# A ring of its own for the convolution LayerNorm's row tiles in a hybrid decoder layer

## The chip, the cores and the metric

The kernel runs on one core of a Trainium2 chip. The metric is the device time of one execution in microseconds (us). The engines are TensorE (PE), VectorE (DVE), ScalarE (ACT), GpSimd (POOL) and SyncE (SP); SP and POOL also issue DMAs. Each engine works through its own queue in order.

## The reference

One sequence of 4096 tokens with 1024 channels goes through one layer, in float32:

```
shift, scale, gate = split(silu(c) @ w_ada + b_ada)
h = layer_norm(x) * (1 + scale) + shift
u_a, z_a, glu_b, z_b = split(h @ w_in + b_in)          # 512, 512, 1024, 512 channels
y_a = (pool(u_a) @ w_pool + b_pool) * ls_pool * silu(z_a)
v = glu_b[..., :512] * sigmoid(glu_b[..., 512:])
v = silu(layer_norm(causal_depthwise_conv_31(v)) * ln_conv_g + ln_conv_b)
y_b = (v @ w_pw + b_pw) * silu(z_b)
y = concat(y_a, y_b) @ w_out + b_out
out = layer_norm(2**0.25 * x + gate * y) * ln_post_g + ln_post_b
```

The convolution has 31 taps for each of 512 channels and reads the current and the 30 earlier tokens. Its LayerNorm runs over the 512 channels of a token.

## The kernel before, in words

The tokens are cut into 8 blocks of T = 512, called sb 0 to 7. Activations are kept with channels on the 128 partitions and tokens along a row, so a tile is [128, 512]. Each matmul product is made of three matmuls: weights and activations are split into a high part and a low part, and high x high, high x low and low x high are added (L346, L347, L348 of `inproj`; L723 to L725 in the pointwise stage; all on L747 in the output projection).

*Phase 1* (the loop at L485) normalises x and makes glu_b and half of z_b. For the next block, `row_stats` (L284) loads four token tiles of x, lets ACT form sums and sums of squares (`col_stats`, L270 and L271) into a tile `xcs` of 8 columns, lets POOL turn the second half into inverse roots (`inv_root`, L274 and L275) and calls `to_rows`: PE transposes the 8 columns into PSUM (tile `xcp`, L74), ACT copies them to a small tile `rows` in SBUF (L281), and SP stores this to DRAM (L282), from where it is read back as a broadcast to all partitions, `xbc` (L293). With it `norm_T` (L301, L303) on DVE and `mod_xT` (L312 on ACT, L313 on DVE) make the normalised x with channels on partitions, `x2`. PE then projects it (tiles p1_sb_n), ACT takes the sigmoid (sg, L464), and DVE multiplies (v, L466); v is stored to DRAM.

*Phase 2* (L534) loads x2 again (DMAs in POOL's queue, L341) and makes the pool mixer: projections p2z, p2u and p2b, window sums on DVE (us, pp).

*The convolution* (L591 to L655) works on v in blocks of one or two sb: (0), (1, 2), (3, 4), (5). All taps run on DVE (L609), channel group by channel group (m = 0 to 3), with accumulators `ca` and scratch `cx` from one ring of six buffers. When the first channel group of the next block has been written in the program, `conv_ln` (L621) of the block before is emitted at high priority: PE transposes the accumulators (tiles cl), ACT forms the statistics `ccs` (L270, L271), POOL the inverse roots (L274, L275), and the same `to_rows` makes rows of them (transpose `ccp`, copy L281). They go through DRAM to a broadcast `cbc` (L637), and DVE normalises the accumulators (L640, L641), which are stored; then the `ca` buffers are free again. Blocks 6 and 7 are "late units" (tiles la, lx, lv), two of which stand ahead of phase 3 and the others between its steps.

*Phase 3* (L689) splits the convolution's output (tiles vp) and the pool mixer's (ya) into high and low (a cast on ACT, L200, and a subtraction on DVE, L201), runs the pointwise projection (pw, L723 to L725), multiplies with z (L730), splits again (yb), and runs the output projection (po, L747) with the weights Wo (loaded and scaled at L784 to L790: DVE L787, ACT L200, DVE L201), then the last LayerNorm.

The program is not run in the order in which it is written. A scheduler walks it with a simulated timeline and puts each instruction into its engine's queue when its operands and buffers would be ready. A buffer comes from a ring: a tag with a number of buffers. A ring gives its buffers out in the order in which the program asks for them, so a tile that is asked for later in the program cannot have a buffer ahead of one that is asked for earlier. All of phase 1 stands ahead of the convolution in the program. The tile `rows` has the tag rows8 with two buffers in both uses of `to_rows`: for x (called with the name `x{sb}`) and for the convolution (called with `c{s0}`).

Of the kernel before, what the change touches and what calls it, by code (L numbers as in the profile page):

```python
# [9 lines left out]
F32 = mybir.dt.float32  # L10
# [7 lines left out]
P = 128  # L18
# [5 lines left out]
TT = T // P  # L24
# [16 lines left out]
def tile_layer(ctx, tc, x, x_t, w_in_t, c, w_ada, b_ada, w_in, b_in, w_pool, b_pool, ls_pool, w_dw, b_dw,  # L41
# [10 lines left out]
    def pool(name, bufs=1, **kw):  # L52
        return ctx.enter_context(tc.tile_pool(name=name, bufs=bufs, **kw))
# [4 lines left out]
    st = pool("st")  # L58
# [13 lines left out]
    def transpose(out_ap, in_ap):  # L72
        n = in_ap.shape[0]
        return nc.tensor.transpose(out_ap, in_ap, ident[:n, :n])  # L74
# [202 lines left out]
    def to_rows(pb, cs, dst, name):  # L277
        n = cs.shape[1]
        transpose(pb[:n, :P], cs)
        rows = st.tile([n, P], F32, tag="rows8", bufs=2, name=f"rows{name}", padded_shape=[4 * TT, P])  # L280
        nc.scalar.copy(rows, pb[:n, :P])  # L281
        nc.sync.dma_start(dst, rows)  # L282

    def row_stats(sb):  # L284
        cs = st.tile([P, 8], F32, tag="cs", bufs=2, name=f"xcs{sb}")
        for t in range(TT):
            i = sb * TT + t
            xt = x_early[t] if sb == 1 else load_x(i)
            col_stats(xt, D, cs[:, t : t + 1], cs[:, 4 + t : 5 + t])
        inv_root(cs[:, 4:8], D)  # L290
        to_rows(tp_bank(f"xcp{sb}"), cs, rD[sb], f"x{sb}")
        bc = ph.tile([P, 2, T], F32, tag="tm", bufs=5, name=f"xbc{sb}")
        nc.sync.dma_start(bc, rD[sb].rearrange("(a t) p -> a (t p)", a=2).partition_broadcast(P))  # L293
        return bc
# [101 lines left out]
    rows = {}  # L396
# [224 lines left out]
    def conv_ln(s0, n, ac):  # L621
        nq = n * TT
        cs = st.tile([P, 2 * nq], F32, tag="ccs", bufs=2, name=f"ccs{s0}", padded_shape=[P, 4 * TT])
        for q in range(nq):
            pb = s2_bank(f"cl{s0}_{q}")
            for m in range(MC):
                transpose(pb[:, m * P : (m + 1) * P], ac[m][:, q * P : (q + 1) * P])
            col_stats(pb, DH, cs[:, q : q + 1], cs[:, nq + q : nq + q + 1])
        inv_root(cs[:, nq : 2 * nq], DH)
        bcs = []  # L630
        to_rows(s2_bank(f"ccp{s0}"), cs, cD[s0][: 2 * nq, :], f"c{s0}")
        for j in range(2):
            if s0 < 6:
                bc = s2.tile([P, n * T], F32, tag="bc", bufs=2, name=f"cbc{s0}_{j}", padded_shape=[P, D])
            else:
                bc = wraw(f"cbc{s0}_{j}")[:, :T]
            nc.sync.dma_start(bc, cD[s0][j * nq : (j + 1) * nq, :].rearrange("q p -> (q p)").partition_broadcast(P))  # L637
            bcs.append(bc)
        for m in range(MC):
            nc.vector.tensor_tensor(ac[m], ac[m], bcs[0], op=ALU.add)  # L640
            nc.vector.scalar_tensor_tensor(ac[m], ac[m], lcg[:, m : m + 1], bcs[1], op0=ALU.mult, op1=ALU.mult)  # L641
            for i in range(n):
                nc.sync.dma_start(tD[m][s0 + i], ac[m].rearrange("p (two i) -> p two i", two=2)[:, :, i * TH : (i + 1) * TH])

    pend = None
    for s0, n in BLOCKS:
        ac = []
        for m in range(MC):
            v = s2.tile([P, 2, HQ + n * TH + 1], F32, tag="cv", bufs=2, name=f"cv{s0}_{m}",
                        padded_shape=[P, 2, HQ + T + 1])  # L650
            a = s2.tile([P, n * T], F32, tag="ca", bufs=6, name=f"ca{s0}_{m}", padded_shape=[P, 2 * (HQ + T + 1)])
            tmp = s2.tile([P, 2 * n * TH + HQ + 1], F32, tag="ca", bufs=6, name=f"cx{s0}_{m}",
                          padded_shape=[P, 2 * (HQ + T + 1)])
# [186 lines left out]
```

## Time and profile before

| | |
|---|---|
| median of 3 runs | 1421.36 us (1421.3 to 1422.22) |
| the profiled execution | 1421.22 us |
| its span in the profile | 1419.4 us |
| mean granted TensorE clock | 0.984 |
| HBM read, written | 156.65 MB, 86.04 MB |
| matmuls on PE | 6109 |

The profile shows one execution. The span goes from the first to the last instruction, and the profiled time is 1.8 us longer. Times in the rows are in us from the span's start. A timeline row has its start, its length, engine, line, operation, output and inputs with their shapes, how many instructions the row stands for, and in brackets how long the engine was idle before it and what ended that wait. A windows row has the stretch, its length, then busy time and instruction count of PE, PE's weight loads, DVE, ACT and POOL, then the granted PE clock (1.00 is full), the share of the DMA engines and GB/s.

### The profile page before, as it was taken

Reading aid. Unit: us, or ns where it says so; the run is one execution under the profiler, and the core shown is the slowest. Engines: PE = TensorE matmul, PEld = TensorE weight load, DVE = VectorE, ACT = ScalarE, POOL = GpSimd, SP = SyncE. Lnnn points to the kernel's source line nnn. Section 1 sums busy time; section 2 is a strip of 40 time slices with the busy share of each in tenths; the row PEclk is TensorE's granted clock in tenths of the full one; section 3 lists DMA queues with packets and bytes.
Section 4 is the critical chain, followed back from the end, with each engine's and each line's share of the span. In section 5 each row is a group of like instructions: output and inputs, shape, how many; then the busy total and the mean of one; then the engine's idle time right before and its main releaser. Section 6 shows DMA issues by size and latency. Waiting matters only on the chain.

```text
span 1419.4 us, 17051 instructions
## 1 busy us (share of the span) xinstructions
PE 1371.0 (97%) x6109; PEld 1129.2 (80%) x6109; DVE 1178.4 (83%) x2220; ACT 432.5 (30%) x772; POOL 115.5 (8%) x159
## 2 busy tenths in 40 slices
PE   5999998999999999999999999987999999999997
PEld 4878886888888888888888888865888888888886
DVE  7588998752419999899999699999998899998754
ACT  3623534245244221321111411243334231323310
POOL 1000003000000001011011010000111001001011
PEclk9999999999999999999999999998999999999999
DMA  9696556456567576164341461436344443343511
GB/s 317 220 313 236 214 187 235 173 208 219 189 233 269 170 220 215 45 203 141 124 157 63 157 212 39 143 122 234 134 149 163 164 155 115 134 154 109 200 63 75
DMA packets 116551, 243.82 MB, mean 172 GB/s; under 512 B 15154, under 2 KB 49778, under 8 KB 116466
## 3 DMA queue, kind: packets, MB, share of 16 engines
q1 hardware_dynamic: 107184, 209.15, 42.5%
q0 software_dynamic: 9216, 33.56, 7.2%
q8 instruction: 48, 0.79, 0.2%
q14 instruction: 37, 0.30, 0.1%
q10 hardware_dynamic: 66, 0.02, 0.0%
HBM read 156.65 MB, written 86.04 MB: 171 GB/s over the span
## 4 chain that ended last, share of the span: by engine, by line
PE 88%; DVE 5%; DMA 3%; ACT 1%; POOL 1%; SPq 1%; issue 1%; DVEq 0%; ACTq 0%; POOLq 0%
PE po L747 24%; PE p L346 7%; PE p L347 7%; PE p L348 7%; PE p2u L347 4%; PE p2z L347 4%; PE p2z L348 4%; PE p2u L348 4%; PE p2u L346 4%; PE p2z L346 4%; PE p2b L348 2%; PE p2b L347 2%; PE p2b L346 2%; PE pw L723 2%; PE pw L725 2%; PE pw L724 2%
## 5 line engine op out<-in xcount | busy, mean ns | idle before, releaser
L609 DVE SCALAR_TENSOR_TENSOR cx<-cv,wdw,cx 128x257 f32<-128x257 f32 (+1 forms) x240 | 145.0, 611 | 1.2
L609 DVE SCALAR_TENSOR_TENSOR ca<-cx,wsum,ca 128x256 f32<-128x256 f32 (+1 forms) x240 | 142.2, 608 | 0.0
L609 DVE SCALAR_TENSOR_TENSOR ca<-cv,wdw,ca 128x256 f32<-128x256 f32 (+1 forms) x224 | 133.9, 608 | 0.0
L466 DVE SCALAR_TENSOR_TENSOR v<-p,cols,sg 128x512 f32<-128x512 f32 x32 | 23.8, 745 | 71.9 <-ACT sg L464 68.9
L770 ACT ACTIVATE ojk<-r,osm 128x1024 bf16<-128x1024 f32 x31 | 35.7, 1151 | 153.4 <-DVE osm L767 153.4
L776 POOL TENSOR_TENSOR ors<-ove,mhalf 128x1 f32<-128x1 f32 x32 | 47.0, 1470 | 398.4 <-DVE ove L772 390.0
L341 POOL DMA_DIRECT2D x2r<-xD x64 | 34.9, 546 | 418.5 <-PE p2b L348 321.8
L539 ACT ACTIVATE sz<-p2z,cols 128x512 f32<-128x512 f32 x32 | 22.0, 688 | 121.8 <-PE p2z L348 113.1
L609 DVE SCALAR_TENSOR_TENSOR lx<-lv,wdw,lx 128x257 f32<-128x257 f32 x120 | 57.5, 479 | 0.0
L765 DVE SCALAR_TENSOR_TENSOR r<-po,r 128x512 f32<-128x512 f32 x62 | 40.6, 685 | 20.4 <-PE po L747 20.4
L609 DVE SCALAR_TENSOR_TENSOR la<-lx,wsum,la 128x256 f32<-128x256 f32 x120 | 57.3, 477 | 0.0
L312 ACT ACTIVATE x<-xk,shc 128x512 fp32r<-128x512 f32 x56 | 38.1, 719 | 59.0 <-DVE xk L303 59.0
L313 DVE SCALAR_TENSOR_TENSOR x<-xk,shc,x 128x512 fp32r<-128x512 f32 x56 | 40.1, 743 | 17.3 <-ACT x L312 17.3
L546 ACT ACTIVATE u<-p2u,bu 128x512 f32<-128x512 f32 x32 | 22.1, 690 | 105.2 <-PE p2u L348 105.2
L609 DVE SCALAR_TENSOR_TENSOR la<-lv,wdw,la 128x256 f32<-128x256 f32 x112 | 53.1, 478 | 0.0
L301 DVE TENSOR_TENSOR xk<-xk,xbc 128x1024 f32<-128x1024 f32 x28 | 34.1, 1218 | 21.8 <-DMA xk<-in_x_t_dram 17.7
L747 PE MATMUL po<-wo0h,ya 128*128 128x512 f32 x128 | 42.0, 400 | 8.6 <-ACT ya L200 8.6
L464 ACT ACTIVATE sg<-p,cols 128x512 f32<-128x512 f32 x32 | 22.0, 687 | 79.5 <-PE p L348 76.7
L200 ACT CAST yb<-z 128x512 fp32r<-128x512 f32 x32 | 19.8, 617 | 81.1 <-DVE z L730 66.4
L779 DVE SCALAR_TENSOR_TENSOR r<-r,ors,b_bc 128x1024 f32<-128x1024 f32 (+1 forms) x33 | 41.1, 1247 | 2.8 <-POOL ors L776 2.8
L747 PE MATMUL po<-wo2h,ya 128*128 128x512 f32 x128 | 40.0, 390 | 0.4 <-ACT ya L200 0.4
L747 PE MATMUL po<-wo1h,ya 128*128 128x512 f32 x128 | 40.3, 390 | 0.0
(378 smaller groups left out, 4107.1 us busy)
## 6 DMA issues: line engine op xcount, KB each, us to landing
x2r<-xD POOLq DMA_DIRECT2D x64, 512.0 KB, 7.5
xD<-x SPq DMA_DIRECT2D x56, 512.0 KB
x<-in_x_dram SPq DMA_DIRECT2D x32, 512.0 KB
r<-in_x_dram SPq DMA_DIRECT2D x32, 512.0 KB
out_dram<-r SPq DMA_DIRECT2D x31, 512.0 KB
xk<-in_x_t_dram SPq DMA_DIRECT2D x28, 512.0 KB
wa<-in_w_ada_dram SPq DMA_DIRECT2D x32, 256.0 KB
vD<-v SPq DMA_DIRECT2D x32, 256.0 KB
```

Source lines behind the costliest of these rows:

```text
L312: nc.scalar.activation(h2[:, 0, :], z, AF.Identity, bias=shc[:, k : k + 1])
L313: nc.vector.scalar_tensor_tensor(h2[:, 1, :], z, shc[:, k : k + 1], h2[:, 0, :].bitcast(F32), op0=ALU.add, op1=ALU.subtract)
L341: nc.gpsimd.dma_start(h2, xD[k][sb].bitcast(F32R))
L346: nc.tensor.matmul(ps, w[0], X[0], start=first, stop=False)
L347: nc.tensor.matmul(ps, w[0], X[1], start=False, stop=False)
L348: nc.tensor.matmul(ps, w[1], X[0], start=False, stop=last)
L609: nc.vector.scalar_tensor_tensor(dst, src, wt, dst, op0=ALU.mult, op1=ALU.add)
L747: mm = nc.tensor.matmul(po[h], lhs, Wo[k][wi][:, h * 512 : (h + 1) * 512], start=(k == 0 and wi == 0 and lhs is yh), stop=last)
L765: nc.vector.scalar_tensor_tensor(r[:, sl], po[h], 1.0, r[:, sl], op0=ALU.mult, op1=ALU.add, accum_out=sm[:, h : h + 1])
L770: nc.scalar.activation(jk, r, AF.Square, bias=sm[:, 2:3], accum_out=ss)
L776: nc.gpsimd.tensor_tensor(rs, ve, mhalf[:, 0:1], op=ALU.pow)
L779: nc.vector.scalar_tensor_tensor(r[:, sl], r[:, sl], rs, b_bc[:, sl], op0=ALU.mult, op1=ALU.add)
```

## The change

The tag of the tile `rows` takes the first letter of its name: `rowsx` for the statistics of x, `rowsc` for those of the convolution. Each has one buffer in place of two shared ones, so the SBUF that they take is the same.

```
@@ -277,7 +277,7 @@
     def to_rows(pb, cs, dst, name):
         n = cs.shape[1]
         transpose(pb[:n, :P], cs)
-        rows = st.tile([n, P], F32, tag="rows8", bufs=2, name=f"rows{name}", padded_shape=[4 * TT, P])
+        rows = st.tile([n, P], F32, tag=f"rows{name[0]}", bufs=1, name=f"rows{name}", padded_shape=[4 * TT, P])
         nc.scalar.copy(rows, pb[:n, :P])
         nc.sync.dma_start(dst, rows)
```

No instruction is added to the arithmetic or taken from it; the scheduler orders the program anew. Up to PE's row 1067 (in sb 4) its queue is the same; the following three places show what differs. In the names, the number behind the tile's own name is the block, and the last number is a running one.

On ACT, in sb 3 of phase 1 (rowsc0 are the rows of convolution block 0, rowsx4 those of x block 4):

```order
 L464 ACTIVATE sg3_1_1958<-p1_3_13_1909,cols_92 128x512
 L281 COPY rowsx4_1838<-xcp4_1836 8x128
+L281 COPY rowsc0_6701<-ccp0_6699 8x128
 L464 ACTIVATE sg3_2_2013<-p1_3_14_1964,cols_92 128x512
 L312 ACTIVATE x2_4_0_2073<-xk4_0_1843,shc_283 128x512
```

The copy of block 0's rows now stands behind that of x block 4; before, it stood directly behind the copy of x block 7 (rowsx7), in sb 6.

On DVE, in sb 4 of phase 1, from the product v4_1 on, before:

```order
L466 SCALAR_TENSOR_TENSOR v4_1_2333<-p1_4_9_2281,cols_92,sg4_1_2331 128x512
L301 TENSOR_TENSOR xk5_0_2216<-xk5_0_2216,xbc5_2214 128x1024
L303 SCALAR_TENSOR_TENSOR xk5_0_2216<-xk5_0_2216,s1n_282,xbc5_2214 128x512 x2
L301 TENSOR_TENSOR xk5_2_2221<-xk5_2_2221,xbc5_2214 128x1024
L313 SCALAR_TENSOR_TENSOR x2_5_0_2446<-xk5_0_2216,shc_283,x2_5_0_2446 128x512
L301 TENSOR_TENSOR xk5_4_2462<-xk5_4_2462,xbc5_2214 128x1024
L466 SCALAR_TENSOR_TENSOR v4_2_2388<-p1_4_10_2336,cols_92,sg4_2_2386 128x512
```

And the same place now (ca1_1, cx1_1, ca1_2 and cx1_2 are the accumulators and scratch of convolution block 1):

```order
L466 SCALAR_TENSOR_TENSOR v4_1_2333<-p1_4_9_2281,cols_92,sg4_1_2331 128x512
L609 SCALAR_TENSOR_TENSOR cx1_1_6722<-cv1_1_6720,wdw_99,cx1_1_6722 128x513
L609 SCALAR_TENSOR_TENSOR ca1_1_6721<-cv1_1_6720,wdw_99,ca1_1_6721 128x512
L609 SCALAR_TENSOR_TENSOR ca1_2_6779<-cx1_2_6780,wsum_100,ca1_2_6779 128x512
L609 SCALAR_TENSOR_TENSOR cx1_2_6780<-cv1_2_6778,wdw_99,cx1_2_6780 128x513
L609 SCALAR_TENSOR_TENSOR ca1_2_6779<-cv1_2_6778,wdw_99,ca1_2_6779 128x512
L609 SCALAR_TENSOR_TENSOR ca1_1_6721<-cx1_1_6722,wsum_100,ca1_1_6721 128x512
```

Nine more taps follow before v4_2, so that fifteen stand between the two products; the first L301 of x block 5 now stands two taps behind v4_2. In the rest of phase 1 taps stand between the norm's instructions in the same way. On PE the transpose xcp5 moves from row 1164 to row 1189 (37 rows behind the last matmul of p1_4_9 and p1_4_13, whose products make v4_1), xcp6 and xcp7 stand at rows 1411 and 1649, and the transposes of the convolution's statistics move from row 2578 to 1982 (ccp1), 3411 to 2868 (ccp3), 4031 to 3466 (ccp5) and hardly for the two late blocks (4604 to 4582, 5560 to 5557). Phase 2 begins at row 2060 in place of 2027.

On PE, where phase 3 begins (pw0_0 and pw0_1 are the first pointwise projections, po0 the first output tile, cl6 a late unit's transpose), before:

```order
L723 MATMUL pw0_0_7802<-vp0_0_7705,wpw0h_7692 128x512
L723 MATMUL pw0_1_7821<-vp0_0_7705,wpw0h_7692 128x512
L74 MATMUL ccp5_7553<-ident_75,ccs5_7522 8x128
L74 MATMUL cl6_0_8676<-ident_75,la6_0_7574 128x128
L74 MATMUL cl6_1_8683<-ident_75,la6_0_7574 128x128
L724 MATMUL pw0_0_7802<-vp0_0_7705,wpw0h_7692 128x512
L725 MATMUL pw0_0_7802<-vp0_0_7705,wpw0l_7693 128x512
L724 MATMUL pw0_1_7821<-vp0_0_7705,wpw0h_7692 128x512
L725 MATMUL pw0_1_7821<-vp0_0_7705,wpw0l_7693 128x512
L747 MATMUL po0_0_7917<-wo0h_7745,ya0_0_7728 128x512
```

And now, from the last matmul of phase 2 on:

```order
L348 MATMUL p2b_7_3_6353<-x2r_7_7_6063,w19l_3628 128x512
L723 MATMUL pw0_0_7802<-vp0_0_7705,wpw0h_7692 128x512
L724 MATMUL pw0_0_7802<-vp0_0_7705,wpw0h_7692 128x512
L725 MATMUL pw0_0_7802<-vp0_0_7705,wpw0l_7693 128x512
L723 MATMUL pw0_0_7802<-vp0_1_7711,wpw0h_7692 128x512
L724 MATMUL pw0_0_7802<-vp0_1_7711,wpw0h_7692 128x512
L725 MATMUL pw0_0_7802<-vp0_1_7711,wpw0l_7693 128x512
L723 MATMUL pw0_0_7802<-vp0_2_7717,wpw1h_7698 128x512
```

The pieces of conv_ln(5) and of the late unit that stood among the first pw matmuls are gone from there, and the pw matmuls of one chunk follow each other.

More of the change, by code (lines that the diff above doesn't have):

```diff
@@ L279, in to_rows @@
         transpose(pb[:n, :P], cs)
-        rows = st.tile([n, P], F32, tag="rows8", bufs=2, name=f"rows{name}", padded_shape=[4 * TT, P])
+        rows = st.tile([n, P], F32, tag=f"rows{name[0]}", bufs=1, name=f"rows{name}", padded_shape=[4 * TT, P])
         nc.scalar.copy(rows, pb[:n, :P])
```

## The prediction

> **What bounds the kernel now.** The page comes first: the span, and what each engine is busy.
>
> ```profile
> span 1419.4 us, 17051 instructions
> PE 1371.0 (97%) x6109; PEld 1129.2 (80%) x6109; DVE 1178.4 (83%) x2220; ACT 432.5 (30%) x772; POOL 115.5 (8%) x159
> ```
>
> The profiled execution took 1421.22 us, 1.8 us more than its span and 0.14 us below the median 1421.36, so I sum against the span and add 1.8. PE is busy 97% of the time: a gain can only come from the 48 us in which it is idle and from stretches at a slow clock. The windows view says where these lie (columns: stretch, length, then PE, weight load, DVE, ACT, POOL busy with their instructions, PE clock, DMA share, GB/s).
>
> ```profile
> 225.00:250.00 25.00, 18.91 (x81) 14.90 (x80) 21.71 (x32) 12.01 (x28) 12.75 (x4) 0.89 0.52 183
> 300.00:400.00 100.00, 100.00 (x462) 83.16 (x461) 35.86 (x47) 35.62 (x59) 2.53 (x4) 1.00 0.59 213
> 925.00:950.00 25.00, 23.50 (x109) 19.30 (x107) 24.33 (x46) 11.48 (x22) 0.00 (x0) 1.00 0.37 117
> 950.00:975.00 25.00, 13.82 (x45) 9.52 (x45) 23.90 (x44) 6.87 (x14) 1.77 (x2) 0.66 0.70 230
> 975.00:1000.00 25.00, 22.16 (x88) 17.26 (x88) 23.73 (x51) 10.60 (x19) 0.00 (x0) 0.93 0.48 164
> 1228.34 21.78 PE po L747 x96
> 947.47 1.04 PE L74 MATMUL cl<-ident,ca 128*128 128x128 f32 x8
> ```
>
> The last row but one, from the chain that ended last, gives PE's full pace: 21.78 / 96 = 0.2269 us per 512-wide matmul; the last one, from PE's timeline, has eight small transposes in 1.04 us, an estimated 0.1 us each. The three slices from 925 to 1000, where phase 2 ends and phase 3 begins, hold 109 + 45 + 88 = 242 matmuls, 13 of them such transposes: 229 x 0.2269 + 1.3 = 53.2 us of work in 75. So 21.8 us are lost there: 25 x 3 - 23.50 - 13.82 - 22.16 = 15.5 idle, the rest slow clock (0.66 and 0.93 in the clock column). PE's timeline shows what it waited for (bracket: idle before, and its releaser), and DVE's what it did meanwhile:
>
> ```profile
> 950.78 0.98 PE L723 MATMUL pw<-vp,wpw0h 128*128 128x512 f32 x2 [2.28 <-ACT vp L200]
> 953.40 0.38 PE L74 MATMUL ccp<-ident,ccs 128*8 128x128 f32 x1 [1.64 <-POOL ccs L275]
> 964.93 1.22 PE L747 MATMUL po<-wo0h,ya 128*128 128x512 f32 x2 [8.62 <-ACT ya L200]
> 985.47 0.79 PE L723 MATMUL pw<-vp,wpw0h 128*128 128x512 f32 x1 [1.66 <-DVE z L730]
> 958.43 2.50 DVE L640 TENSOR_TENSOR ca<-ca,cbc 128x512 f32<-128x512 f32 x4 [0.36 <-DMA cbc<-cD]
> 964.22 2.73 DVE L641 SCALAR_TENSOR_TENSOR ca<-ca,lcg,cbc 128x512 f32<-128x512 f32 x4
> ```
>
> The 8.62 us wait is the largest. DVE is full there (23.90 of 25): the conv LayerNorm of block 5 (5.2 us in the last two rows) and taps stand in DVE's queue between PE and the splits (vp, ya) that it needs. Yet in 300 to 400 the same engine is busy for only 35.86 of 100 us, although conv taps were still to be done. Why, these rows show:
>
> ```profile
> 246.49 0.38 PE L74 MATMUL ccp<-ident,ccs 128*8 128x128 f32 x1 [4.50 <-POOL ccs L275]
> 412.98 0.26 ACT L281 COPY rowsx<-xcp 8x128 f32<-8x128 f32 x1 [3.31 <-PE xcp L74]
> 413.14 0.25 ACT L281 COPY rowsc<-ccp 8x128 f32<-8x128 f32 x1
> 421.88 2.49 DVE L640 TENSOR_TENSOR ca<-ca,cbc 128x512 f32<-128x512 f32 x4 [0.26 <-DMA cbc<-cD]
> ```
>
> Block 0's transposed statistics are ready at 246.5, but their copy to rows runs at 413.14, right behind that of x block 7: the shared ring hands buffers out in program order, and conv_ln(0) stands behind all of phase 1 there. Until 421.88 block 0's accumulators are not given back, and conv runs dry.
>
> **The change part by part.** *What goes.* With its own buffer rowsc0 is copied directly behind rowsx4, near 247 us. No arithmetic is added; the rings hold the same bytes. The conv taps fill DVE from about 250 on, and conv_ln runs earlier: ccp5 moves from PE's row 4031 to row 3466, 565 x 0.2269 = 128 us. In the new order the pw matmuls stand without a break behind phase 2, and nothing of conv_ln(5) or the late units stands around them on DVE. So the 21.8 us go, but for a rest: out projection still needs z through L730, a cast and a split (1.66 us above) and the Wo weights. I leave 2 us (0 to 5).
>
> *What earlier conv work buys elsewhere.* Nothing: PE is busy for all 25 us of every slice from 250 to 925, the first and last of which are
>
> ```profile
> 250.00:275.00 25.00, 25.00 (x109) 20.53 (x108) 16.56 (x25) 6.87 (x10) 0.00 (x0) 0.97 0.22 78
> 900.00:925.00 25.00, 25.00 (x112) 20.68 (x112) 24.97 (x51) 7.43 (x10) 0.00 (x0) 1.00 0.37 117
> ```
>
> The 6.1 us idle in 225 to 250 lie ahead of the first PE row that the change moves and stay.
>
> *What it adds.* From 300 to 425 the norm of x (L301 to L313) had DVE to itself; now it shares DVE with gapless 512-wide taps. Each x block's statistics pass through POOL (L274, L275) to a transpose in PE's queue; behind that transpose all of PE waits. The rows:
>
> ```profile
> 233.52 4.50 POOL L274 TENSOR_SCALAR xcs<-xcs 128x4 f32<-128x4 f32 x1 [60.34 <-ACT x L271]
> 237.86 0.75 DVE L466 SCALAR_TENSOR_TENSOR v<-p,cols,sg 128x512 f32<-128x512 f32 x1
> 239.20 0.27 PE L74 MATMUL xcp<-ident,xcs 128*8 128x128 f32 x1 [1.58 <-POOL xcs L275]
> 239.13 6.19 POOL L274 TENSOR_SCALAR ccs<-ccs 128x4 f32<-128x4 f32 x1
> 243.81 0.75 DVE L609 SCALAR_TENSOR_TENSOR ca<-cv,wdw,ca 128x512 f32<-128x512 f32 x1
> 244.48 0.75 DVE L609 SCALAR_TENSOR_TENSOR ca<-cx,wsum,ca 128x512 f32<-128x512 f32 x1
> 245.40 1.04 POOL L275 TENSOR_TENSOR ccs<-ccs,mhalf 128x4 f32<-128x4 f32 x1
> 246.52 0.77 PE L347 MATMUL p<-x,wg3h 128*128 128x512 f32 x1
> 251.36 0.40 PE L346 MATMUL p<-x,wg5h 128*128 128x512 f32 x1
> 300.31 0.23 POOL L274 TENSOR_SCALAR xcs<-xcs 128x4 f32<-128x4 f32 x1 [53.88 <-ACT x L271]
> ```
>
> L274 takes 0.23 us beside an idle DVE, but 4.50 and 6.19 inside streaks of 512-wide taps at 0.67 us pitch; the first ended when DVE ran an operation from PSUM (L466), the second when the streak ended at 245.2. PE lost 1.58 and 4.50 us, and after the longer one its 11 matmuls from 246.52 to 251.36 took 4.84 us for 11 x 0.2269 = 2.50: 2.3 more.
>
> Now xcs5. On ACT the last L271 of x block 5 now stands behind sg4_1, and xcp5 stands 37 PE rows, 8.4 us, behind the matmuls of that chunk. So POOL starts some 2.0 us behind the chunk (sg 0.69, L271 1.14 and its readout 0.19):
>
> ```profile
> 299.00 1.14 ACT L271 ACTIVATE x<-x,xcs 128x1024 f32<-128x1024 f32 x1
> 300.04 0.19 ACT L271 ACTIVATION_READ_ACCUMULATOR x<-x,xcs 128x1 f32 x1
> 301.43 0.69 ACT L464 ACTIVATE sg<-p,cols 128x512 f32<-128x512 f32 x1 [1.21 <-PE p L348]
> ```
>
> DVE runs v4_1 from 0.7 to 1.5 and then 15 taps without a break, 10 us, to 11.5. L274 ends there, L275 1.04 later, at 12.5: 4.1 us late, with the slow clock 6.4; if POOL gets in between two taps, 0. I take 5.
>
> The Trainium skill, SBUF — State Buffer, "SBUF: two separate sides", says that a DVE operation with two SBUF inputs and a GpSimd operation that reads SBUF take their shared ports as an exclusive lock, held for a whole instruction. By it POOL would enter behind one tap (0.75 us), xcs5 would cost nothing and the time would be 5 us less; 4.50 and 6.19 span seven and nine taps, so I go by the trace.
>
> xcs6 is ready some 4.5 us behind the chunk of v5_0, and xcp6 stands 47 rows, 10.7 us, behind that chunk; v5_1 comes between and lets POOL in: 0 to 1. xcs7 waits through 15 taps for v6_1, about 1.2 us behind its chunk, and takes L275's 1.04 more; xcp7 stands three rows, 0.7 us, behind that chunk: 1.5 to 2. ccs1 has ten us to its transpose, and among the splits of weights that wait for ACT's casts DVE has gaps: 0 to 1. The new rows are as late for norm_T as the transposes: before, from xcp5 (303.73) to x2_5_0's lo half took 12.0 us:
>
> ```profile
> 303.73 0.27 PE L74 MATMUL xcp<-ident,xcs 128*8 128x128 f32 x1
> 312.54 1.41 DVE L303 SCALAR_TENSOR_TENSOR xk<-xk,s1n,xbc 128x512 f32<-128x512 f32 x2
> 313.88 1.22 DVE L301 TENSOR_TENSOR xk<-xk,xbc 128x1024 f32<-128x1024 f32 x1
> 315.01 0.75 DVE L313 SCALAR_TENSOR_TENSOR x<-xk,shc,x 128x512 fp32r<-128x512 f32 x1
> ```
>
> Now 12 taps (8.0), two more L301 (2.3), three more L303 pairs (4.0) and v4_3 (0.7) stand ahead of it: 27.0. PE wants it 116 rows, 26.3 us, behind xcp5: 0 to 3, I take 1. At the start of phase 2 eight operations of conv_ln(1) stand ahead of v7_1, whose PSUM bank p2z waits for: 0 to 2, I take 1. POOL's queue now has conv_ln(1)'s pair between reloads 5 and 6 of the first x block, and SP's has its stores and broadcasts among phase 2's weight loads; what is queued behind them is first used at PE's row 2060, 78 rows or 17.7 us behind ccp1, which covers a wait of 6.19 on POOL: 0. Were that cover gone, it would be those 6 us.
>
> Sum: 5 + 2 + 1 + 1 = 9 us added, from 0 to about 20. Span 1419.4 - 21.8 + 2 + 9 = 1408.6, time **1410.4 us**.
>
> **The rivals.** *POOL decides (slower).* All four POOL pairs that now fall among taps (xcs5, xcs6, xcs7, ccs1) wait out a full streak: 6.19 + 2.3 = 8.5 us each, 34 in all, so 1421.2 - 21.8 + 2 + 34 = 1435 us. From 5 us per event up it eats the gain (19.8 / 4). For: two of two cases among 512-wide taps. Against: it needs each to start early in a streak and its transpose to stand close behind; by the order that holds for xcs5 only. 0.07.
>
> *The hole stays (same).* The 8.62 us wait names ya, but the Wo weights go into slots that phase 2's last chunks free, and if they come as late PE waits for them instead:
>
> ```profile
> 961.24 1.22 DVE L201 TENSOR_TENSOR wo7l<-wor,wo7h 128x1024 fp32r<-128x1024 f32 x1
> ```
>
> Then 8.62 + 2.3 of slow restart, 11 us, stay in place of my 2: 1410.4 + 9 = 1419.4, and up to 1424 where POOL costs 5 more than I took. For: wo7 is split at 961, next to that wait. Against: po begins with wo0, which was split earlier, and the splits now pass a DVE that is rid of 5.2 us of conv_ln and of the taps. 0.10.
>
> *Full gain.* POOL enters between the taps, as a 0.38 us L274 among 256-wide taps says:
>
> ```profile
> 171.60 0.38 POOL L274 TENSOR_SCALAR xcs<-xcs 128x4 f32<-128x4 f32 x1 [48.07 <-ACT x L271]
> ```
>
> Then only 0 to 3 us are added: 1400 to 1405. 0.20.
>
> *No effect.* If accumulators or another ring still held conv back, the order would not move; it does, by 128 us at ccp5. 0.01.
>
> **How the numbers follow.** The forecast has 0.62. A measurement can tell 0.2%, 2.8 us, from no change. The range, 1400 to 1422, has the full gain at its low end and the hole that stays at its high end; it leaves out POOL's 0.07, 0.05 of the hole's and the forecast's upper ends (20 us added) and 0.05 for a gain beyond 1400. Faster (below 1418.5): 0.62 + 0.20, less 0.02 of the forecast for its upper end: 0.80. Slower (above 1424.2): 0.07 and 0.03 of the hole's: 0.10. Same: the hole's other 0.07, the 0.02 and the 0.01: 0.10.
>
> **What would show it.** Right: rowsc0 copied near 247; DVE over 95% from 250 to 425; PE 24 or more of 25 in the slices where phase 2 ends, and no wait for ya or vp of over 2 us; a L274 of some 8 us near 303 to 313 with a PE wait of 4 for xcs behind it. Wrong: PE waits at the end of phase 2 adding up to over 8 us (the hole stays); each of the four L274 over 5 us with PE waits behind them (POOL decides); all of them under 1 us (full gain).

## The result and the profile after

The changed kernel takes 1410.78 us (median of 4 runs, 1409.85 to 1412.63) against 1421.33 for the kernel before on the same occasion (1421.22 to 1422.22): ratio 0.9926, with a 95% interval of 0.9909 to 0.9943. That is 10.6 us faster. The profiled execution took 1412.63 us, the longest of the four, 8.6 less than the profiled one of before; its span is 8.5 shorter. The page:

```profile
span 1410.9 us, 17053 instructions
PE 1370.4 (97%) x6109; PEld 1129.3 (80%) x6109; DVE 1181.7 (84%) x2220; ACT 435.7 (31%) x774; POOL 127.0 (9%) x159
```

PE's idle time fell from 48.4 to 40.5 us, and the work is the same. The windows view shows the stretch where phase 2 ends, and three rows from where conv was idle (columns as before):

```profile
925.00:950.00 25.00, 25.00 (x112) 20.70 (x111) 16.45 (x21) 7.16 (x10) 0.00 (x0) 1.00 0.32 106
950.00:975.00 25.00, 25.00 (x111) 20.59 (x110) 14.35 (x19) 6.77 (x9) 0.00 (x0) 1.00 0.55 178
975.00:1000.00 25.00, 25.00 (x112) 20.66 (x111) 24.91 (x54) 8.00 (x14) 1.54 (x1) 1.00 0.42 149
350.00:375.00 25.00, 22.98 (x96) 18.52 (x95) 21.79 (x35) 10.48 (x18) 2.04 (x2) 0.93 0.64 234
300.00:400.00 100.00, 97.98 (x446) 80.92 (x445) 96.19 (x144) 38.70 (x60) 3.73 (x4) 0.98 0.56 201
400.00:425.00 25.00, 23.00 (x97) 18.57 (x96) 23.74 (x36) 15.72 (x24) 6.44 (x2) 0.93 0.53 191
```

The hole is gone: 25.00 of 25 at full clock in all three slices, with DVE down from 24 to 14 to 16 us in two of them. The work has moved to where DVE was idle: in 300 to 400 it is now busy for 96.2 us (before 35.86). In exchange PE now loses some in 350 to 375 and 400 to 425, where before it lost nothing. What PE waited for in all (us, times, longest), from the waits view, without the waits at the kernel's start that before has too:

```profile
PE xcp L74 <- POOL xcs L275: 5.3, 3, 2.0
PE ccp L74 <- POOL ccs L275: 4.5, 1, 4.5
...
PE p2u L346 <- DVE v L466: 2.8, 1, 2.8
...
PE p2z L346 <- ACT sg L464: 1.1, 1, 1.1
```

The waits for ya, vp and z at the change of phase are gone. New are two of the three for xcs (before had one, 1.58 us) and those of p2u and p2z, at the start of phase 2. Their places, from PE's timeline, with the first matmul at full pace behind each of the longer ones:

```profile
362.51 0.27 PE L74 MATMUL xcp<-ident,xcs 128*8 128x128 f32 x1 [2.02 <-POOL xcs L275]
366.74 0.40 PE L346 MATMUL p<-x,wg4h 128*128 128x512 f32 x1
421.16 0.27 PE L74 MATMUL xcp<-ident,xcs 128*8 128x128 f32 x1 [2.00 <-POOL xcs L275]
424.92 0.39 PE L346 MATMUL p<-x,wg2h 128*128 128x512 f32 x1
513.93 0.50 PE L346 MATMUL p2z<-x2r,w4h 128*128 128x512 f32 x1 [1.09 <-ACT sg L464]
522.42 0.50 PE L346 MATMUL p2u<-x2r,wu0h 128*128 128x512 f32 x1 [2.75 <-DVE v L466]
527.33 0.40 PE L348 MATMUL p2u<-x2r,wu0l 128*128 128x512 f32 x1
```

Behind xcp6 11 matmuls take 4.2 us in place of 2.5, behind xcp7 nine take 3.7 in place of 2.0, behind p2u 14 take 4.9 in place of 3.2: 1.7 us of slow clock each time, from eight matmuls at 0.43 us in place of 0.23. So the change costs 2.0 + 1.7 (xcs6), 2.0 + 1.7 (xcs7) and 1.1 + 2.75 + 1.7 (phase 2): 12.95 us, against 21.8 gained. 8.85 is the sum, and the spans of these two executions differ by 8.5 (the medians by 10.6).

### The profile page after: what moved, and what is told of

Its sections match the earlier page's. It is cut to its first block, busy times and chain, and to the rows that moved or that the text cites. A ratio compares the mean times of both kernels' runs of the same rounds, so it can differ in the third digit from the quotient of the medians.

```text
span 1410.9 us, 17053 instructions
## 1 busy us (share of the span) xinstructions
PE 1370.4 (97%) x6109; PEld 1129.3 (80%) x6109; DVE 1181.7 (84%) x2220; ACT 435.7 (31%) x774; POOL 127.0 (9%) x159
## 4 chain that ended last, share of the span: by engine, by line
PE 82%; DVE 6%; DMA 6%; ACT 2%; POOL 2%; SPq 1%; issue 1%; DVEq 0%; ACTq 0%; POOLq 0%
PE po L747 25%; PE p L346 5%; PE p L347 5%; PE p L348 5%; PE p2u L346 4%; PE p2u L348 4%; PE p2u L347 4%; PE p2z L348 4%; PE p2z L347 4%; PE p2z L346 4%; PE pw L725 2%; PE pw L723 2%; PE pw L724 2%; PE p2b L348 2%; PE p2b L346 2%; PE p2b L347 2%
## 5 line engine op out<-in xcount | busy, mean ns | idle before, releaser
L776 POOL TENSOR_TENSOR ors<-ove,mhalf 128x1 f32<-128x1 f32 x32 | 48.4, 1511 | 440.0 <-DVE ove L772 431.6
L274 POOL TENSOR_SCALAR xcs<-xcs 128x4 f32<-128x4 f32 x7 | 12.3, 1754 | 380.1 <-ACT x L271 380.1
L301 DVE TENSOR_TENSOR xk<-xk,xbc 128x1024 f32<-128x1024 f32 x28 | 34.2, 1220 | 12.1 <-DMA xk<-in_x_t_dram 12.1
L739 DVE SCALAR_TENSOR_TENSOR r<-r,gbo 128x1024 f32<-128x1024 f32 x32 | 39.1, 1221 | 4.7 <-DMA r<-in_x_dram 4.7
```

Source lines behind the costliest of these rows:

```text
L739: xg = nc.vector.scalar_tensor_tensor(r, r, ALPHA, gbo, op0=ALU.mult, op1=ALU.add)
L776: nc.gpsimd.tensor_tensor(rs, ve, mhalf[:, 0:1], op=ALU.pow)
```

## The experiments

The theory: the whole gain lies in when rowsc0 may be copied, since that lets conv fill an idle DVE early and empties DVE where phase 2 ends; what it costs comes from GpSimd being locked out by gapless taps, and from conv_ln(1) meeting the start of phase 2. Rivals are named in each expectation. Medians of the kernel before stood at 1419.88 to 1420.03 us beside these runs, so ratios are compared, and the changed kernel's is 0.9926.

### Only the moment of the copy put back (e_hold7)

```
+        if name == "c0":
+            after(cp, row_copies["x7"])      # cp = nc.scalar.copy(rows, ...)
```

> The changed kernel with its two rings, but the copy of rowsc0 is made to stand behind that of rowsx7 on ACT. Theory (all of the change lies in when that copy may run): the time of the kernel before, 1421 us, with the hole of some 22 us at 925 to 1000 back and no wait for xcs6 and xcs7. Rival (something else about the rings or the new order, such as where the buffers lie): it keeps the time of the changed kernel, 1411.

Measured: 1419.38 us, ratio 1.0 (0.999 to 1.0011). PE's waits are those of before, the longest one, at the change of phase, among them:

```profile
PE po L752 <- ACT ya L200: 8.7, 1, 8.7
```

Two rings, with this one copy behind rowsx7, are the kernel before. Nothing else about the rings plays a part; the rival falls.

### A copy that is only half as late (e_hold5)

The same edit with `row_copies["x5"]`.

> The changed kernel with the copy of rowsc0 made to stand behind that of rowsx5, so that the taps of block 1 start some 55 us later than in it. Theory (VectorE has time to spare: 10 to 16 of 25 us from 875 to 975): the hole stays closed; conv_ln(1) falls behind phase 1 (ccp1 behind the first p2z), so the waits for p2z and p2u (5.5 us) go and the wait for xcs7 remains: 1404 to 1408. Rival (the earlier start is what counts, every us of delay costs): 1414 to 1418.

Measured: 1409.21 us, ratio 0.9921 (0.9907 to 0.9934), the same as the changed kernel's and 1.2 us above the range. The hole stays closed (25.00 of 25 in every slice from 900 to 1000), so an earlier start by 55 us is not worth anything of itself. The waits changed places instead of going: those for p2z and p2u are gone as expected, but xcs6 now waits out a streak of taps, and PE waits 3.4 us for ACT's statistics of conv_ln:

```profile
355.08 6.11 POOL L274 TENSOR_SCALAR xcs<-xcs 128x4 f32<-128x4 f32 x1 [53.04 <-ACT x L271]
362.37 0.27 PE L74 MATMUL xcp<-ident,xcs 128*8 128x128 f32 x1 [2.66 <-POOL xcs L275]
```

Behind this wait of 2.66 us no matmul ran slow: the granted clock from 350 to 375 was 1.00.

### Is the hole a full VectorE? (e_early0)

The kernel before, with two late units moved from ahead of phase 3 to between its output tiles; the ring is left shared.

```
-EARLY = 2
-PERSB = (1, 1, 1, 1, 1, 1, 0, 0)
+EARLY = 0
+PERSB = (2, 2, 1, 1, 1, 1, 0, 0)
```

> The kernel before, its shared ring untouched, with the two late units that stood ahead of phase 3 moved between its first output tiles, one more behind each of sb 0 and sb 1. Theory (the hole of 21.8 us is a VectorE that is too full at the change of phase): most of the hole goes although conv_ln(0) still waits until 413 us; 1401 to 1408, if phase 3 can hide the 37 us of taps more. Rival (the Wo weights or PE's own order make the hole): it stays, 1418 to 1422.

Measured: 1423.63 us, ratio 1.0026 (1.0017 to 1.0035). The time is wrong for the theory and the profile is right for it. The windows of this kernel:

```profile
925.00:950.00 25.00, 25.00 (x112) 20.51 (x112) 22.56 (x33) 9.87 (x16) 1.27 (x2) 1.00 0.64 205
950.00:975.00 25.00, 25.00 (x111) 20.61 (x110) 19.67 (x34) 11.54 (x19) 0.00 (x0) 1.00 0.76 263
...
1325.00:1350.00 25.00, 19.69 (x91) 15.81 (x89) 14.59 (x29) 7.96 (x20) 3.68 (x4) 0.97 0.29 105
1350.00:1375.00 25.00, 9.62 (x30) 6.48 (x31) 9.80 (x15) 6.61 (x11) 0.48 (x1) 0.62 0.32 105
```

The hole at 925 to 1000 is gone without any change to the ring, so the Wo weights did not make it: the taps that stood ahead of phase 3 did. But not by a full DVE alone, which is still busy for 22.56 and 19.67 of 25 us here while PE never waits. What also changed is that conv_ln(5) comes 22 us earlier: its rows are stored at 932.04 (954.10 before), while PE still has phase 2 to do. These rows of the kernel before show how conv_ln(5) holds PE (the last is from the waits of SP's queue):

```profile
960.95 0.32 SPq L710 DMA_DIRECT2D ya<-yD  x1
964.26 1.14 ACT L200 CAST ya<-ya 128x512 fp32r<-128x512 f32 x2 [2.53 <-DMA ya<-yD]
SPq L710 <- DVE ca L640: 2.6, 1, 2.6
```

The first ya takes its buffer from the same ring `bc` as cbc (L634, L709), so its load waits until block 5's last L640 has read cbc (960.93), then the cast waits for the load and PE for the cast. Of the 17 us from conv_ln(5)'s transposes (947.47) to the first po matmul (964.93) DVE takes 2.5; the rest is the way of the statistics through ACT, POOL, PE and DRAM, and ya's load and cast. The waits of 2.28 (a vp cast behind conv_ln(5)'s statistics on ACT), 1.64 (ccp5) and 8.62 us, 12.5 of the 15.5 idle, belong to this chain. Only behind them do the splits on a full DVE hold PE (1.66 us for z among others). The edit also takes late units' transposes out of PE's queue there, which was not tested by itself.

But a hole as large opens at 1325 to 1375, where PE waits 14.5 us for vp of the last block: conv was not started earlier, so the same DVE work came too late elsewhere. The gain of the change is not that it empties one place, but that it uses DVE time that lay idle.

### GpSimd out of the path (e_sqrt, e_before_sqrt, e_roots, e_adddve)

```
-        nc.gpsimd.tensor_scalar(ss, ss, n * EPS, None, op0=ALU.add)
-        nc.gpsimd.tensor_tensor(ss, ss, mhalf[:, : ss.shape[1]], op=ALU.pow)
+        nc.scalar.activation(ss, ss, AF.Sqrt)
+        nc.vector.reciprocal(ss, ss)
```

> The changed kernel with the inverse roots off GpSimd: a square root on ACT and a reciprocal on VectorE, which leaves out the epsilon. Theory (GpSimd is locked out by taps): PE's waits for xcs at 238.8, 362.5 and 421.2 us and for ccs at 246 us go with the slow clock behind them, 8 + 7.4 us, less some for ACT's table loads: 1395 to 1400 us. Rival (the statistics are late on ACT, not on GpSimd): the waits stay and the time is 1409 to 1413.

Measured: 1397.51 us, ratio 0.9842 (0.9826 to 0.9857). No wait for xcs or ccs is left in the list. The same edit in the kernel before:

> The kernel before with the inverse roots off GpSimd (square root on ACT, reciprocal on VectorE, without the epsilon). Theory (before lost only 1.3 + 4.5 + 2.3 us to the lock near 240 us and 1.6 us at ccp5, and keeps its hole of 21.8 us): 1410 to 1414 us, so that the ring alone is worth 13 to 17 us between two kernels without GpSimd in the path (1397.5 with it). Rival (the gain of the version off GpSimd is general, as large without the ring change as with it, 13 us): 1406 to 1408.

Measured: 1409.98 us, ratio 0.9925 (0.9907 to 0.9942). The hole is still there, and now the largest wait of the kernel:

```profile
PE po L747 <- ACT ya L200: 12.3, 1, 12.3
```

So the two edits nearly add: 10 us for GpSimd alone, 10.6 for the ring alone, 22.5 for both; between the two kernels without GpSimd the ring is worth 12.5 us, a little under the 13 to 17 expected. With the epsilon, and so with the whole computation (square root with the epsilon as its bias):

> The changed kernel with the whole computation and the inverse roots off GpSimd: square root with the epsilon as its bias on ACT, reciprocal on VectorE. The same time as without the epsilon, 1396 to 1399 us; faster than both kernels. If the bias or a table load costs more: up to 1402.

Measured: 1401.3 us (1397.71 to 1403.99), ratio 0.9864 (0.9844 to 0.9884); above the 1396 to 1399, within its second case. Last, only the addition moved, `nc.vector.tensor_scalar` for L274, the power left on GpSimd:

> The changed kernel with only the addition L274 on VectorE; the power L275 stays on GpSimd and is now the operation that arrives there. If taps lock out any operation of GpSimd that reads SBUF: L275 lasts 3 to 7 us among them at least twice, waits for xcs and ccs stay, 1407 to 1413. If it is only the form of L274: L275 keeps 1.04 to 1.4 us and the time falls to 1397 to 1400.

Measured: 1394.79 us, ratio 0.9815 (0.9798 to 0.9833): faster than both kernels and the lowest median of all that were run, with the whole computation. The expectation's two cases both missed it. GpSimd's rows (the three for x blocks 5 to 7 are alike, the last is shown):

```profile
233.69 3.36 POOL L275 TENSOR_TENSOR xcs<-xcs,mhalf 128x4 f32<-128x4 f32 x1 [57.37 <-DVE xcs L274]
...
410.00 1.38 POOL L275 TENSOR_TENSOR xcs<-xcs,mhalf 128x4 f32<-128x4 f32 x1 [55.13 <-DVE xcs L274]
```

The power was held once (3.36 us against 1.02 beside an idle DVE) and otherwise 0.36 us. Coming behind a small DVE operation, it always arrives at about the same point of a tap: 0.25 us into it where it was held, 0.23 or 0.24 where it got in. One thing stays mixed in: in the three versions of the changed kernel in this section the scheduler also puts the transposes later on PE (xcp6 at row 1421 or 1427, xcp7 at 1669, against 1411 and 1649), which gives 2 to 4.5 us of room. How much of the gain is the missing lock and how much that room was not separated.

### The lock by itself (p_lock, p_phase)

> A probe that leaves out the whole layer: GpSimd runs 160 operations like L274 ([128, 4], one by one) while VectorE runs four streaks without a wait in them: 36 taps of 512 with both inputs in SBUF, 60 taps of 256, 36 one-input multiplications of 512, 36 taps of 512 with one input in PSUM. The lock theory: among the 512-wide SBUF taps a GpSimd operation lasts over 2 us, up to the streak's end (24 us), among the PSUM taps 0.23 to 0.5 us. The one-tap rule of the Trainium skill (SBUF, two separate sides): at most about 0.9 us each among SBUF taps of 512 and 0.6 among those of 256. No lock at all: 0.23 us everywhere, and the long L274 had another cause.

The probe's windows (DVE busy, then GpSimd busy; the four lines are from the streaks of 512-wide SBUF taps, 256-wide SBUF taps, one-input multiplications and PSUM taps):

```profile
25.00:30.00 5.00, 5.00 (x10) 5.00 (x9) 1.00 0.00 0
35.00:40.00 5.00, 5.00 (x14) 5.00 (x14) 1.00 0.00 0
60.00:65.00 5.00, 5.00 (x14) 5.00 (x14) 1.00 0.00 0
70.00:75.00 5.00, 5.00 (x9) 2.94 (x16) 1.00 0.02 2
```

One GpSimd operation for each tap in the first three, and 0.18 us each beside PSUM taps: the one-tap rule, and not the theory. But these operations all come right behind one another, at the same point of a tap. So:

> A second probe that leaves out the layer: two gapless streaks of taps on VectorE as in conv (240 of 513, 512, 512 and 150 of 257, 256, 256 columns, three accumulators in turn), while 40 operations like L274 on GpSimd are each released by an ACT operation of changing length, so that they arrive at different points of a tap. In the first probe each came directly behind the last one and lasted one tap (0.66 us). If the point of arrival decides whether GpSimd gets in at the next tap or waits on: durations under 0.9 us for some and over 3 us for others among the 512-wide taps. If the one-tap rule holds whatever the phase: all under 0.9 us, and the 4.50, 6.19 and 5.40 us in the kernel need another reason.

DVE's streak of 390 taps, and of GpSimd's rows the first, the fifth and sixth, and the one behind the streak:

```profile
5.78 218.54 DVE L60 SCALAR_TENSOR_TENSOR acc<-src,wt,acc 128x513 f32<-128x513 f32 x390
6.76 0.51 POOL L68 TENSOR_SCALAR cs<-cs 128x4 f32<-128x4 f32 x1 [6.34 <-ACT cs L67]
...
12.32 0.25 POOL L68 TENSOR_SCALAR cs<-cs 128x4 f32<-128x4 f32 x1 [1.07 <-ACT cs L67]
13.69 210.71 POOL L68 TENSOR_SCALAR cs<-cs 128x4 f32<-128x4 f32 x1 [1.12 <-ACT cs L67]
225.56 0.22 POOL L68 TENSOR_SCALAR cs<-cs 128x4 f32<-128x4 f32 x1 [1.16 <-ACT cs L67]
```

Five operations get in at the end of the tap in which they arrive, each a little later in its tap than the one before (they last 0.51 us down to 0.25, against 0.22 behind the streak); the sixth arrives 0.61 us into a tap of 0.66 us pitch and is held until the last of 390 taps, for 210.71 us, though hundreds of boundaries pass, those of the 256-wide taps too. So both are true: an operation either gets in at the next boundary or is starved for as long as the streak lasts. Which it will be is not settled, and the point of arrival alone does not decide it. In the probe 0.32 to 0.57 us into a tap got in; in the kernels 0.18 got in (360.33) and 0.09, 0.31 and 0.61 did not. And in e_lnlate (the next section) an operation that came 0.40 us into a tap was held past the boundary at 303.14, until v4_1 ran at 303.81:

```profile
302.88 1.10 POOL L274 TENSOR_SCALAR xcs<-xcs 128x4 f32<-128x4 f32 x1 [56.97 <-ACT x L271]
```

### The start of phase 2 (e_lnlate, e_rowslate, e_rl_sqrt)

```
+            if s0 == 1 and m == 0:
+                after(ln_add, last_v[0])     # ln_add: L640's instruction, last_v: v7_3's
```

> The changed kernel, with one order added: conv_ln(1)'s first L640 stands behind the last product of phase 1, v7_3, on VectorE. Theory: PE's waits of 1.09 us (p2z, for sg) and 2.75 us (p2u, for v) and the slow clock behind them, 5.5 us in all, go: 1405 us. Rival: the products were late for another reason (casts of weights that wait for DMAs in the same queue), and the waits stay: 1410 to 1411.

Measured: 1414.32 us, ratio 0.9957 (0.9942 to 0.9972): no faster than the changed kernel, and slower in the median. The edit held only the first of the four L640 behind v7_3; the other three still ran ahead, so it does not settle the theory. The wait for v is gone, and the one that names the sigmoid has grown:

```profile
PE p2z L346 <- ACT sg L466: 6.3, 1, 6.3
```

The changed kernel's rows from SP, ACT and DVE tell where its two waits come from:

```profile
498.14 0.57 SPq L282 DMA_DIRECT2D cD<-rowsc  x1
502.56 0.81 SPq L637 DMA_DIRECT2D cbc<-cD  x2
503.79 0.32 SPq L377 DMA_DIRECT2D wru<-uD  x1
512.24 1.05 ACT L200 CAST wu3h<-wru 128x1024 fp32r<-128x1024 f32 x1 [8.77 <-DMA wru<-uD]
513.20 0.68 ACT L464 ACTIVATE sg<-p,cols 128x512 f32<-128x512 f32 x1
508.69 4.63 DVE L640 TENSOR_TENSOR ca<-ca,cbc 128x1024 f32<-128x1024 f32 x4 [5.39 <-DMA cbc<-cD]
521.62 0.74 DVE L466 SCALAR_TENSOR_TENSOR v<-p,cols,sg 128x512 f32<-128x512 f32 x1
```

SP issues the store of rowsc1 and then stands 4.4 us at the broadcast, until the store has landed; behind it in the queue is a weight load, behind whose cast on ACT the sigmoid of v7_1 stands, and the sigmoid's bank is the one that p2z needs. That is the wait of 1.09 us. The wait of 2.75 us is for v7_1 itself, whose bank p2u needs: its sigmoid was done at 513.88, but v7_1 ran only at 521.62, behind the eight operations of conv_ln(1) on DVE, which had waited for the broadcast until 508.69. Test: the copy of rowsc1 behind the last sigmoid, which takes the broadcast from ahead of the load and the eight operations from ahead of v7_1.

```
+        if name == "c1":
+            after(cp, last_sg[0])            # sg7_3
```

> The changed kernel, with conv_ln(1)'s copy of rowsc1 made to stand behind the last sigmoid of phase 1 (sg7_3) on ACT, so that its store and broadcast leave SP's queue between the weight loads of phase 2. Theory (SP held at the broadcast until the store had landed, and with it the weight load whose cast stands ahead of sg7_1 on ACT): PE's waits before p2z and p2u (3.84 us and the slow clock behind, 5.5 us in all) go; 1405 to 1406 us. Rival (the casts and the splits of the weights are late by themselves): the waits stay, 1410 to 1411.

Measured: 1404.44 us, ratio 0.9894 (0.9874 to 0.9914), 0.6 us below the theory's range. The waits for sg and v are gone (0.2 us of p2z is left, for a reload). The run moves both causes at once and does not separate SP's queue from DVE's order; only the rows above do. GpSimd's lock and this order together:

> Both together: inverse roots off GpSimd (without the epsilon) and rowsc1 behind sg7_3. If the two causes add: the time of the kernel with the roots off GpSimd, 1397.5, less its waits for p2z and p2u (1.7 + 1.9 us and some slow clock): 1393 to 1394 us. If the waits stay: 1397 to 1398.

Measured: 1397.08 us, ratio 0.9841 (0.9827 to 0.9855), the same as without GpSimd alone: there PE still waits 1.9 us for the sigmoid. In that order the sigmoid stands behind casts of weights and a table load that are late by themselves; the causes don't add.

## Why the prediction was right, point by point

*The time* came out 0.4 us from the forecast, in good part by luck. The forecast kept 11 us back from the 21.8 (9 added and 2 of rest). Of these, 8 did not come (xcs5, the rest, the late norm); the other three cost 12.95 us in place of 3. And by the profiled execution the gain was 8.5, not 10.6.

*What goes (21.8 us, less 2).* Right in place and size: the hole closed wholly, the rest of 2 us isn't there. e_hold7 shows that the copy's moment is all of it, e_early0 that conv's late work made the hole. The way was in part another than I wrote: the 8.62 us were not the queue on DVE ahead of ya's split, but the way of conv_ln(5)'s statistics and the ring `bc` that cbc and ya share. The rival "the hole stays" falls: the Wo weights were in time. Of the signs, rowsc0 was copied at 246.46, and DVE was over 95% busy from 300 to 400 (96.2) but not from 250 to 300 (42.7 of 50 us).

The statistics of x blocks 5, 6 and 7 in the timeline of the changed kernel:

```profile
302.59 0.65 POOL L274 TENSOR_SCALAR xcs<-xcs 128x4 f32<-128x4 f32 x1 [56.59 <-ACT x L271]
303.06 0.75 DVE L466 SCALAR_TENSOR_TENSOR v<-p,cols,sg 128x512 f32<-128x512 f32 x1
346.72 1.06 ACT L270 ACTIVATE x<-x 128x1024 f32<-128x1024 f32 x1 [7.27 <-DMA x<-in_x_dram]
360.33 0.65 POOL L274 TENSOR_SCALAR xcs<-xcs 128x4 f32<-128x4 f32 x1 [55.98 <-ACT x L271]
414.59 5.40 POOL L274 TENSOR_SCALAR xcs<-xcs 128x4 f32<-128x4 f32 x1 [52.13 <-ACT x L271]
```

*xcs5 (5 us).* The step that failed. By the order L274 was to come behind v4_1 and wait through 15 taps. It came at 302.59, while v4_1 itself ran late at 303.06; L274 took 0.65 us, to 0.18 us behind the start of v4_1 (which reads PSUM), and PE did not wait. I had put v4_1 at the first moment its operands were there, on a DVE that I myself called full.

*xcs6 (0 to 1) and xcs7 (1.5 to 2).* 3.7 us each. xcs7's place was right: L274 lasted 5.40 us, until v6_1. I had left out the slow clock, since 1.58 us of waiting had cost none before; here 2.00 did, and yet 2.66 in e_hold5 did not, so the length of a wait alone does not say. xcs6's wait is another one than I looked for: ACT waited for x loads, and the last L271 ended only at 360.2. The last of these loads was issued at 345.44 (339.37 before), in SP's queue between stores of x2 that wait for the norm on the fuller DVE. POOL among the taps added 0.8 us (L274 0.65 in place of 0.23, L275 1.39 in place of 1.04).

*The late norm (1 us).* No wait at the start of p1_5: 0.

*The start of phase 2 (1 us) and SP's queue (0).* 5.5 us. The larger part, 2.75 and 1.7 of slow clock, is the term that I had at 1: the operations of conv_ln(1) ahead of v7_1, which themselves came late; it is p2u that waits for them. The other 1.1 us is SP's queue. That what is queued there is "first used at PE's row 2060", so that ccp1's distance covers it, was wrong: I looked at who uses the weights on PE, not at who stands behind their casts on ACT. In e_rowslate both are gone.

*The rival "POOL decides"* needed 5 us from each of four events. One of the four was held for over 5 us, and cost 3.7 us. *"Full gain"* was the better guess for three of the four L274 (0.65, 0.65 and, for ccs1, 0.55 us), though v4_1 let the first one in; the other two got in between operations with two SBUF inputs. Here the Trainium skill, SBUF — State Buffer, "SBUF: two separate sides" (the loser waits until the other's instruction ends), fits p_lock and those two, and does not fit 5.40 us in the kernel and 210.71 in the probe.

## What to carry to other kernels

Two unrelated uses of one small ring can couple stages that lie hundreds of microseconds apart: where an engine is idle while work for it exists, look for a buffer that is handed out in program order. Here there were two such rings: rows8, and bc, through which a late LayerNorm held the first load of phase 3. Earlier work is only worth the hole that it closes, and it must be placed on an engine's idle time: what it then shares a queue with (statistics for PE, loads behind a waiting broadcast) is where part of the gain goes. When you trace a moved wait, follow each queue it stands in to the operation behind it, not only to the one that uses its data.

## What the runs showed of the hardware

A small GpSimd operation that reads SBUF can be starved by a gapless streak of two-input VectorE operations for as long as the streak lasts (210.71 us in the probe, 4.50 to 6.19 in the kernels), and not only for one instruction; an operation with a PSUM input, or a gap, let it in. Others got in at the next boundary, within 0.25 to 0.65 us, and no run here tells what decides. In the changed kernel waits of 2.00, 2.02 and 2.75 us on TensorE were followed by eight matmuls each at 0.43 us in place of 0.23, one of 1.29 us by none; in e_hold5 one of 2.66 us was followed by none, so the length alone does not decide that either.
